# Step-wise inverses and layer norm, and projections that pass once over their weights, in a hybrid DeltaNet and sliding-window block

## The chip, the cores and the metric
One core of one Trainium2 chip (trn2). The metric is the device time of one execution in microseconds, as the median of several runs. The profile was taken in an execution of its own.

## The reference, cut to what matters
One post-norm block on x (1, 2048, 1024) in float32. Two token mixers read the same projections: a gated DeltaNet with 4 heads of 128 (chunks of the delta rule with a triangular inverse), and sliding-window attention with 8 query heads of 64 (window 128, rotation of the first quarter of each head). Both are gated, projected, merged, projected once more, added to the input and layer-normalized.

```python
h = einsum("bsd,dc->bsc", x, w_in)
t_inv = triangular_solve(eye + lower, eye)
u = t_inv @ (v * beta); w = t_inv @ (k_beta * exp(g))
def step(state, xs):
    v_new = u_i - w_i @ state
    o_i = qd_i @ state + a_i @ v_new
    state = state * exp(gl_i) + kt_i.T @ v_new
q_b = partial_rope(sw_q, cos, sin)
y_b = banded_sink_attention(q_b, k_b, v_b, sinks) * silu(sw_z)
merged = sigmoid(gate_a) * (y_a @ w_branch[0]) + sigmoid(gate_b) * (y_b @ w_branch[1])
r = DEEPNORM_ALPHA * x + merged @ w_out
y = (r - mean(r)) * rsqrt(var(r) + LN_EPS) * ln_g + ln_b
```

## The kernel before, in words
The 2048 tokens are worked on in four chunks of 512 (T), each of four blocks of 128 (NB). Every large product is made of three matmuls (L175, L176, L177 in `prods`): both operands are split into a high and a low part, and the product of the two low parts is dropped. The weights come as tiles `wb` of 512 KB (high and low part), in four buffers; in chunk 0 they are loaded raw and split by ScalarE (L156) and GpSimd (L157), and kept in DRAM as `kw_...` (one name for each kind: `kw_q` query, `kw_o` output projection, `kw_h` heads, `kw_g` gates), from which later chunks load them (L152).

The order of the work on TensorE is written by hand. A string names the pieces of a chunk ("kv k0 k1 q0 v0 p p p q1 p g w0 v1 z0 ... w1 v3 ..."), which are dense projections: `q0` projects queries of DeltaNet head 0, `p` is a quarter of the output projection of the chunk before (`project`), `w0` and `w1` are the query projections of the window attention (`window_q`) with two gate projections each, `g` is a gate. Between their matmuls a small planner (class `Order`) sets the steps of sparse tasks. It has a virtual clock, `st.now`, which each step moves on by what it costs TensorE. A task that was spawned runs again when its latency has passed on that clock; `until` lets a task wait for another one, and `finish` moves the clock on to whichever task is due, with no dense work in between, until the named task is done. The queues of the other engines are ordered by the scheduler, from the order in which the code emits.

The sparse tasks of a head: `front` (transposes L389 and products up to the matrix `m2`, whose diagonal parts go to DRAM and come back as `su`, L400 to L402); `inverse` (32x32 triangular inverses on VectorE: a memset at L905 as the first reader of `su`, then L908 to L910 and 16 pairs L916/L917; the result goes out at L425); `levels` (loads it back as `p_`, L437, and builds up the large inverse, first matmul L449); `back`, the delta chain (L496 matmul S k, L498 `bt` on VectorE, L501/L504 matmuls, L503 `wc` on VectorE, L507/L509 matmuls, L508 new state `S` on VectorE, and again for each of four blocks); `delta_gate`. For the window attention `query_rows` transposes the rotated queries (L564), and `attend` uses them.

`window_q` and `project` go twice over their weights: a first pass over two blocks loads four `wb` tiles and keeps them, a second pass over the other two blocks uses them again. `window_q` rotates the queries of two blocks behind each pass (`rope`, L866 to L868 on VectorE). `project` adds the input (L681); after the last quarter `layer_norm` of the chunk before is emitted as a whole: statistics on VectorE (L699), the normalization on ScalarE (L701), scale and shift on GpSimd (L708, L709) with parameters loaded as `s` (L705), and the store (L712). The layer norm of the last chunk has code of its own.

Of the kernel before, what the change touches and what calls it, by code (L numbers as in the profile page):

```python
# [16 lines left out]
P = 128  # L17
D = 1024
KT = D // P
T = 512  # L20
# [41 lines left out]
def build(tc, xt, xn, wk, wg, par, lnp, cst, out, seq=2048):  # L62
    nc = tc.nc
    NCH = seq // T
    with ExitStack() as ctx:
# [103 lines left out]

        def prods(ps, terms, first=True, last=True):  # L170

            n = len(terms) - 1
            cost = PE_R * ps.free_size() / 512
            for i, (sh, sl, mh, ml) in enumerate(terms):
                nc.tensor.matmul(ps, sh, mh, start=(first and i == 0), stop=False)  # L175
                nc.tensor.matmul(ps, sh, ml, start=False, stop=False)  # L176
                nc.tensor.matmul(ps, sl, mh, start=False, stop=(last and i == n))  # L177
                if cost * 3 * (i % 2 + 1) > 1000 or i == n:
                    yield cost * 3 * (i % 2 + 1)
# [12 lines left out]
        def prod_tc(pss, blocks, ah, al, ww, load=None):  # L192

            for g, (wh, wl) in enumerate(ww):
                if load:
                    load(2 * g + 1)
                for ps, b in zip(pss, blocks):
                    yield from prods(ps, [(tok(ah[2 * g + k], b), tok(al[2 * g + k], b), wh[:, k], wl[:, k])
                                          for k in range(2)], g == 0, g == 3)

        def kept(ww, into):
# [221 lines left out]
        def inverse(h, su, xi):  # L423
            small_inverse(tc, pt.tile([P, 256], F32, name="xt"), su, xi.rearrange("p (c i) -> p c i", i=32))
            nc.sync.dma_start(out=at(scr_p[h % 2], 0, [[P, P], [1, P]]), in_=xi)  # L425
            yield 0, 0

        def levels(c, h, m2, q_):

            yield from st.until(f"front{h}")  # L430
            if h:
                yield from st.until(f"levels{h - 1}")
            p_ = pt.tile([P, NB, 64], F32, name="p_")
            nc.gpsimd.memset(p_[:32, :, 32:], 0.0)
# [105 lines left out]
        def window_q(c, gp):  # L540

            if gp:
                st.finish("window0")
            c.qT = [pa.tile([P, NB, 2, P], F32R, name=n, bufs=1) for n in ("qT0", "qT1")]
            ww, more = [], quarters([f"q{gp}{i}" for i in range(2)])
            for b0 in (0, 2):
                pss = [mm.tile([P, T], F32, name="mm")[:, :256] for _ in range(2)]
                yield from prod_tc(pss, (b0, b0 + 1), c.xh, c.xl, ww if b0 else kept(more, ww), lambda k: load_x(c, k))
                if b0:
                    st.finish("qT0")  # L550
                qr = [pa.tile([P, 256], F32, name="kr") for _ in range(2)]
                for b, ps in enumerate(pss):
                    rope(nc, sm, qr[b], ps, 4, cos[:, c.i * NB + b0 + b], sin[:, c.i * NB + b0 + b])
                st.spawn(f"qT{b0}", query_rows(c, b0, qr), LAT_Q)
            for g in range(2):
                yield from silu2(c, f"zb{2 * gp + g}")
            st.spawn(f"window{gp}", attend(c, gp), LAT_W)
# [15 lines left out]
        def attend(c, gp):  # L573
            for b0 in (0, 2):
                yield from st.until(f"qT{b0}")
            if not gp:
                c.yBh = py.tile([P, 4, T], F32R, name="yBh")
                c.yBl = py.tile([P, 4, T], F32R, name="yBl")
# [88 lines left out]
        def project(c, eg):  # L667

            if not eg:
                c.ra = [py.tile([P, 2, D], F32, name=n) for n in ("yBh", "yBl")]  # L670
            ww, more = [], quarters([f"o{eg}{i}" for i in range(2)])
            es = slice(256 * eg, 256 * eg + 256)
            xr, pss = [], [mm.tile([P, 2, 256], F32, name="mm") for _ in range(2)]
            for bp in range(2):
                xr.append(pa.tile([P, 2, 256], F32, name="s"))
                t0 = c.i * T + bp * 256
                nc.sync.dma_start(out=xr[bp], in_=xn[t0:t0 + 256, es].rearrange("(b p) e -> p b e", p=P))
            for b2 in range(2):
                yield from prod_tc([ps[:, b2] for ps in pss], (b2, 2 + b2), c.mh, c.ml, ww if b2 else kept(more, ww))
            for bp in range(2):  # L680
                nc.vector.scalar_tensor_tensor(c.ra[bp][:, :, es], xr[bp], 2.0 * ALPHA, pss[bp], ALU.mult, ALU.add)  # L681

        def norm_factors(c, bst):
            mv = sm.tile([P, 2], F32, name="mv")
            nc.vector.bn_aggr(mv, bst)
            va = sm.tile([P, 1], F32, name="va")
            nc.vector.tensor_scalar(va, mv[:, 1:2], 4.0e-5, None, ALU.add)
            rs = sm.tile([P, 1], F32, name="rs")
            rsqrt(nc, sm, rs, va, mhalf)
            nm = sm.tile([P, 1], F32, name="lnm")  # L690
            nc.vector.scalar_tensor_tensor(nm, mv[:, 0:1], -1.0, rs, ALU.mult, ALU.mult)
            return rs, nm

        def layer_norm(c):
            for b in range(NB):
                r = c.ra[b // 2][:, b % 2]
                bst = sm.tile([P, 4, 6], F32, name="st", bufs=1)[:, :2]
                for i in range(2):
                    nc.vector.bn_stats(bst[:, i], r[:, 512 * i:512 * i + 512])  # L699
                rs, nm = norm_factors(c, bst)  # L700
                nc.scalar.activation(r, r, AF.Identity, scale=rs, bias=nm)  # L701
            for eg in range(4):
                es = slice(256 * eg, 256 * eg + 256)
                lg = pa.tile([P, 2, 256], F32, name="s")
                nc.sync.dma_start(out=lg, in_=bass.AP(tensor=lnp.tensor, offset=lnp.offset + 256 * eg, ap=[[0, P], [D, 2], [1, 256]]))  # L705
                for bp in range(2):
                    r = c.ra[bp][:, :, es]
                    nc.gpsimd.tensor_tensor(r, r, lg[:, 0:1].to_broadcast([P, 2, 256]), ALU.mult)  # L708
                    nc.gpsimd.tensor_tensor(r, r, lg[:, 1:2].to_broadcast([P, 2, 256]), ALU.add)  # L709
            for bp in range(2):  # L710
# [49 lines left out]
        def piece(c, w):  # L760
# [6 lines left out]
            elif w == "p":  # L767
                e = next(c.projects)
                st.dense([project(c.prev, e)])
                if e == 3:  # L770
                    layer_norm(c.prev)
            elif w[0] == "w":
# [33 lines left out]
class Order:  # L806

    def __init__(self):  # L810
        self.now, self.tasks, self.done = 0.0, [], set()
# [5 lines left out]
    def step(self, t):  # L817
        try:
            dur, lat = next(t[2])
        except StopIteration:  # L820
            self.done.add(t[1])
            self.tasks.remove(t)
            return
        self.now += dur
# [74 lines left out]
def small_inverse(tc, t, su, xi):  # L899
# [6 lines left out]
    for m in range(0, 16, 8):  # L906
        ms = slice(m, m + 8)
        nc.vector.tensor_tensor(tm, rows[:, ms, 1], view(su, 66 * m + 1, [[66, 8], [0, 32]]), ALU.mult)  # L908
        nc.vector.tensor_tensor(rows[:, ms, 0], rows[:, ms, 0], tm, ALU.add)
    nc.vector.memset(view(su, 0, [[33, 32]]), 1.0)  # L910
    tx = t.rearrange("p (c r k) -> p c r k", r=2, k=32)
    for i in range(30, -1, -2):
# [3 lines left out]
        nc.vector.tensor_tensor(tx[:, :, :, :n], u, x, ALU.mult)  # L916
        nc.vector.tensor_reduce(xi[:, :, i:i + 2], tx[:, :, :, :n], AX.X, ALU.add)  # L917


# [72 lines left out]
```

## Time and profile before

| what | value |
|---|---|
| median of 3 runs | 1720.17 us (1720.06 to 1723.12) |
| profiled execution | 1723.25 us |
| its span | 1721.5 us |
| mean granted TensorE clock | 0.983 of full speed |
| TensorE busy | 1631.3 us, 95% of the span |
| VectorE busy | 1020.2 us, 59% |
| ScalarE busy | 547.8 us, 32% |
| GpSimd busy | 374.2 us, 22% |
| DMA | 323.39 MB, 188 GB/s in the mean |

The profile shows one execution. PE is TensorE, DVE is VectorE, ACT is ScalarE, POOL is GpSimd, SP the engine whose queue issues most transfers; L12 is line 12 of the kernel. In a row of a timeline the first number is the start in microseconds from the start of the span, the second the duration, and the square brackets at the end give the idle time of the engine before it and what ended it. The releaser of a wait is inferred from semaphore events.

### The profile page before, as it was taken

How to read it: one execution, taken by the hardware profiler on the slowest of the kernel's cores; microseconds unless marked ns; L12 is line 12 of the kernel's file. 1: busy time of each engine (PE TensorE's matmuls, PEld its weight loads, DVE VectorE, ACT ScalarE, POOL GpSimd, SP SyncE). 2: the span in 40 equal slices, each digit the busy share in tenths (PEclk: the TensorE clock that was granted, in tenths of full speed). 3: DMA queues.
4: the chain of work that ended last, by engine and by line, in shares of the span. 5: the costliest groups of instructions: out<-in, count | busy, mean ns of one | idle time of the engine just before them, and what ended most of it. 6: DMA issues, size and time to landing. Idle time of an engine off the chain costs nothing.

```text
span 1721.5 us, 27328 instructions
## 1 busy us (share of the span) xinstructions
PE 1631.3 (95%) x9846; PEld 1372.2 (80%) x9846; DVE 1020.2 (59%) x3118; ACT 547.8 (32%) x1496; POOL 374.2 (22%) x366
## 2 busy tenths in 40 slices
PE   8989999999897999999989899999998989999997
PEld 6867878778886878888888687888888868888787
DVE  5677678446757756435546765643554867463245
ACT  3454445333232532321303243323130334333100
POOL 4543454341334111010003311100010521100002
PEclk9999999999999999999999999999999999999999
DMA  8765675667685455557555645556656554464862
GB/s 301 241 219 193 209 245 190 216 204 237 204 251 186 130 168 167 142 165 240 176 167 172 205 133 159 159 152 191 190 167 213 176 168 142 145 189 141 279 204 80
DMA packets 189159, 323.39 MB, mean 188 GB/s; under 512 B 31072, under 2 KB 45408, under 8 KB 188896
## 3 DMA queue, kind: packets, MB, share of 16 engines
q1 hardware_dynamic: 185184, 316.40, 58.3%
q0 software_dynamic: 3840, 5.25, 1.4%
q8 instruction: 78, 1.28, 0.3%
q14 instruction: 57, 0.47, 0.1%
HBM read 244.97 MB, written 71.37 MB: 184 GB/s over the span
## 4 chain that ended last, share of the span: by engine, by line
PE 71%; DVE 13%; DMA 9%; issue 3%; ACT 2%; SPq 1%; POOL 1%; ACTq 0%; DVEq 0%; POOLq 0%
PE mm L175 19%; PE mm L177 18%; PE mm L176 18%; DVE xt L916 2%; DMA wb<-kw_o 2%; PE pp L627 2%; DVE kr L867 2%; PE pp L619 1%; DVE xi L917 1%; DMA w<-in_wg 1%; DMA su<-scrm 1%; DMA wb<-kw_kv 1%; PE pp L588 1%; PE pp L589 1%; PE pd L501 1%
## 5 line engine op out<-in xcount | busy, mean ns | idle before, releaser
L175 PE MATMUL mm<-xh,wb 128*128 128x512 f32 x1128 | 474.4, 421 | 0.9 <-DMA wb<-kw_h 0.9
L177 PE MATMUL mm<-xh,wb 128*128 128x512 f32 x1128 | 447.1, 396 | 0.0
L176 PE MATMUL mm<-xl,wb 128*128 128x512 f32 x1128 | 446.2, 396 | 0.0
L177 PEld LDWEIGHTS mm<-xh,wb 128*128 128x128 f32 x1128 | 213.5, 189 | 50.2
L175 PEld LDWEIGHTS mm<-xh,wb 128*128 128x128 f32 x1128 | 214.6, 190 | 44.6 <-issue 5.7
L176 PEld LDWEIGHTS mm<-xl,wb 128*128 128x128 f32 x1128 | 215.2, 191 | 35.6
L157 POOL TENSOR_TENSOR wb<-w,wb 128x512 fp32r<-128x512 f32 (+1 forms) x110 | 149.7, 1362 | 193.2 <-ACT wb L156 171.2
L175 PE MATMUL mm<-wb,s 128*128 128x256 f32 x384 | 113.2, 295 | 18.7 <-DMA wb<-kw_o 12.9
L175 PE MATMUL mm<-wb,xh 128*128 128x256 f32 (+1 forms) x384 | 115.1, 300 | 11.0 <-DVE rope L866 4.2
L176 PE MATMUL mm<-wb,s 128*128 128x256 f32 x384 | 109.9, 286 | 1.0 <-POOL wb L157 1.0
L176 PE MATMUL mm<-wb,xh 128*128 128x256 f32 (+1 forms) x384 | 110.1, 287 | 0.3 <-POOL wb L157 0.3
L177 PE MATMUL mm<-wb,s 128*128 128x256 f32 x384 | 109.7, 286 | 0.0
L177 PE MATMUL mm<-wb,xl 128*128 128x256 f32 (+1 forms) x384 | 109.6, 285 | 0.0
L156 ACT ACTIVATE wb<-w 128x512 fp32r<-128x512 f32 (+1 forms) x110 | 68.8, 629 | 115.8 <-PE mm L177 55.7
L916 DVE TENSOR_TENSOR xt<-su,xi 128x16 f32<-128x16 f32 (+15 forms) x256 | 99.4, 388 | 5.5
L175 PEld LDWEIGHTS mm<-wb,s 128*128 128x128 f32 x384 | 74.4, 194 | 22.9 <-DMA wb<-kw_o 15.4
L605 ACT ACTIVATE s<-s,nm 128x256 f32<-128x256 f32 (+1 forms) x128 | 62.7, 491 | 82.6 <-DVE nm L599 82.6
L175 PEld LDWEIGHTS mm<-wb,xh 128*128 128x128 f32 x384 | 74.0, 193 | 14.3 <-issue 6.3
L917 DVE TENSOR_REDUCE xi<-xt 128x8 f32<-128x16 f32 (+15 forms) x256 | 74.6, 291 | 5.9
L176 PEld LDWEIGHTS mm<-wb,s 128*128 128x128 f32 x384 | 74.3, 194 | 1.6 <-POOL wb L157 1.5
L176 PEld LDWEIGHTS mm<-wb,xh 128*128 128x128 f32 x384 | 74.0, 193 | 0.9 <-POOL wb L157 0.6
L177 PEld LDWEIGHTS mm<-wb,s 128*128 128x128 f32 x384 | 74.2, 193 | 0.0
(666 smaller groups left out, 3165.4 us busy)
## 6 DMA issues: line engine op xcount, KB each, us to landing
wb<-kw_h SPq DMA_DIRECT2D x96, 512.0 KB, 4.1
wb<-kw_g SPq DMA_DIRECT2D x96, 512.0 KB, 4.0
w<-in_wg SPq DMA_DIRECT2D x106, 256.0 KB, 4.1
wb<-kw_b SPq DMA_DIRECT2D x48, 512.0 KB, 4.6
wb<-kw_o SPq DMA_DIRECT2D x36, 512.0 KB, 4.9
kw_h<-wb SPq DMA_DIRECT2D x32, 512.0 KB, 3.9
kw_g<-wb SPq DMA_DIRECT2D x32, 512.0 KB, 3.4
wb<-kw_q SPq DMA_DIRECT2D x24, 512.0 KB, 4.0
```

Source lines behind the costliest of these rows:

```text
L156: nc.scalar.activation(hi, raw, AF.Copy)
L157: nc.gpsimd.tensor_tensor(lo, raw, hi.bitcast(F32), ALU.subtract)
L175: nc.tensor.matmul(ps, sh, mh, start=(first and i == 0), stop=False)
L176: nc.tensor.matmul(ps, sh, ml, start=False, stop=False)
L177: nc.tensor.matmul(ps, sl, mh, start=False, stop=(last and i == n))
L501: nc.tensor.matmul(ps, q_[:, b], bt, start=True, stop=True)
L588: nc.tensor.matmul(psc[v][:, g, k0:], c.qT[v][:, b, g], kT[v][:, ks], start=True, stop=False)
L605: nc.scalar.activation(s[:, g, k0:], s[:, g, k0:], AF.Exp, bias=nm[:, g:g + 1], scale=0.125, accum_out=su[:, g:g + 1])
L627: nc.tensor.matmul(psY[64 * v:64 * v + 64], c.vs[b + kb][:, 64 * v:64 * v + 64], pTs[v][:, kb], start=(kb == kbs[0]), stop=(kb == 1))
L867: nc.vector.tensor_tensor(d[:, :, 0:8], a[:, 0, :, 0], a[:, 1, :, 1], ALU.subtract)
L916: nc.vector.tensor_tensor(tx[:, :, :, :n], u, x, ALU.mult)
L917: nc.vector.tensor_reduce(xi[:, :, i:i + 2], tx[:, :, :, :n], AX.X, ALU.add)
```

## The change
Four things change.

- `prod_all` takes the place of the two passes in `window_q` and `project`. It goes once over the weights; for each tile it runs over the four blocks in the order 0, 2, 1, 3, with two blocks open in each of two PSUM banks.
- In `window_q` the ropes of all blocks and both spawned `query_rows` come after the whole projection. `st.finish("qT0")` stands directly behind the spawning of qT0, which is due 7.9 us later on the virtual clock (LAT_Q).
- `inverse` and `layer_norm` yield after each step with `None` as cost, by which the virtual clock is not moved, and a latency after which the next step is emitted. `levels` waits for `inverse`, and `attend` for `norm`.
- `layer_norm` (chunks 0 to 2, run in chunks 1 to 3) applies its factors with 32 `scalar_tensor_tensor` of 128x256 on VectorE, in place of 4 activations on ScalarE and 16 instructions of 128x512 on GpSimd.

```diff
+        def prod_all(pss, ah, al, ww, load=None):
+            for g, (wh, wl) in enumerate(ww):
+                if load:
+                    load(2 * g + 1)
+                for b in (0, 2, 1, 3):
+                    yield from prods(pss[b // 2][:, b % 2], [(tok(ah[2 * g + k], b), tok(al[2 * g + k], b), wh[:, k], wl[:, k])
+                                                             for k in range(2)], g == 0 and not b % 2, g == 3, True)
...
         def inverse(h, su, xi):
-            small_inverse(tc, pt.tile([P, 256], F32, name="xt"), su, xi.rearrange("p (c i) -> p c i", i=32))
+            yield from small_inverse(tc, pt.tile([P, 256], F32, name="xt"), su, xi.rearrange("p (c i) -> p c i", i=32))
             nc.sync.dma_start(out=at(scr_p[h % 2], 0, [[P, P], [1, P]]), in_=xi)
-            yield 0, 0
+            yield None, 0
         def levels(c, h, m2, q_):
...
+            yield from st.until(f"inverse{h}")
...
             c.qT = [pa.tile([P, NB, 2, P], F32R, name=n, bufs=1) for n in ("qT0", "qT1")]
-            ww, more = [], quarters([f"q{gp}{i}" for i in range(2)])
+            pss = [mm.tile([P, 2, 256], F32, name="mm") for _ in range(2)]
+            yield from prod_all(pss, c.xh, c.xl, quarters([f"q{gp}{i}" for i in range(2)]), lambda k: load_x(c, k))
             for b0 in (0, 2):
-                pss = [mm.tile([P, T], F32, name="mm")[:, :256] for _ in range(2)]
-                yield from prod_tc(pss, (b0, b0 + 1), c.xh, c.xl, ww if b0 else kept(more, ww), lambda k: load_x(c, k))
                 if b0:
                     st.finish("qT0")
                 qr = [pa.tile([P, 256], F32, name="kr") for _ in range(2)]
-                for b, ps in enumerate(pss):
-                    rope(nc, sm, qr[b], ps, 4, cos[:, c.i * NB + b0 + b], sin[:, c.i * NB + b0 + b])
+                for b in range(2):
+                    rope(nc, sm, qr[b], pss[b0 // 2][:, b], 4, cos[:, c.i * NB + b0 + b], sin[:, c.i * NB + b0 + b])
                 st.spawn(f"qT{b0}", query_rows(c, b0, qr), LAT_Q)
...
             if not gp:
+                if c.i:
+                    yield from st.until("norm")
...
-            for b2 in range(2):
-                yield from prod_tc([ps[:, b2] for ps in pss], (b2, 2 + b2), c.mh, c.ml, ww if b2 else kept(more, ww))
+            yield from prod_all(pss, c.mh, c.ml, quarters([f"o{eg}{i}" for i in range(2)]))
...
-                rs, nm = norm_factors(c, bst)
-                nc.scalar.activation(r, r, AF.Identity, scale=rs, bias=nm)
+                rs, mu = norm_factors(c, bst, NB)
+                fs.append((r, rs, mu))
+                yield None, 2500
...
-                for bp in range(2):
-                    r = c.ra[bp][:, :, es]
-                    nc.gpsimd.tensor_tensor(r, r, lg[:, 0:1].to_broadcast([P, 2, 256]), ALU.mult)
-                    nc.gpsimd.tensor_tensor(r, r, lg[:, 1:2].to_broadcast([P, 2, 256]), ALU.add)
+                for r, rs, mu in fs:
+                    nc.vector.scalar_tensor_tensor(r[:, es], r[:, es], mu, lg[:, 0], ALU.subtract, ALU.mult)
+                    nc.vector.scalar_tensor_tensor(r[:, es], r[:, es], rs, lg[:, 1], ALU.mult, ALU.add)
+                    yield None, 1800
...
-                    layer_norm(c.prev)
+                    st.spawn("norm", layer_norm(c.prev), 0)
...
     def step(self, t):
...
+        if dur is None:
+            t[0] += lat
+            return
```

In `small_inverse` a `yield None, 1800` stands after each of the two steps L908/L909, and a `yield None, 420 + 40 * n` after each of the 16 pairs L916/L917 (n is 2, 4, ... 32).

The lines move with the change: L175 to L177 become L176 to L178, L496 L507, L498 L509, L501 L512, L503 L514, L504 L515, L507 L518, L508 L519, L509 L520, L564 L574, L866 to L868 L884 to L886, L905 L923, L908/L909 L926/L927. The two instructions of the new layer norm are L721 and L722.

How instructions move, at three places. First, TensorE in chunk 2, at the end of the query projection of w1 (the 128x256 matmuls are the projection, those of 128x512 a gate projection, `pd` are products of the delta chain, `pp<-ct,kr` the transposes of the rotated queries). Before:

```order
L175 MATMUL mm<-wb,xh 128x256
L176 MATMUL mm<-wb,xh 128x256
L177 MATMUL mm<-wb,xl 128x256
L564 MATMUL pp<-ct,kr 128x128 x4
L175 MATMUL mm<-xh,wb 128x512
L176 MATMUL mm<-xl,wb 128x512
L177 MATMUL mm<-xh,wb 128x512
...
L501 MATMUL pd<-bt,q__10757 128x128
L504 MATMUL pd<-S,qd 128x128
L175 MATMUL mm<-xh,wb 128x512
```

With the change:

```order
L177 MATMUL mm<-wb,xh 128x256
L178 MATMUL mm<-wb,xl 128x256
L507 MATMUL pd<-S,k 128x128
L512 MATMUL pd<-bt,q__10764 128x128
L515 MATMUL pd<-S,qd 128x128
L518 MATMUL pd<-wc,ktl 128x128
L520 MATMUL pd<-wc,dt 128x128
L507 MATMUL pd<-S,k 128x128
L574 MATMUL pp<-ct,kr 128x128 x4
L176 MATMUL mm<-xh,wb 128x512
```

The steps of a block of the chain and the transposes now stand behind each other, with no dense matmul in between. In w0 of chunks 1 to 3 five such products stand ahead of the transposes. Farther on, the first L449 of head 1 (during w0's gate projections and what follows) stands behind 30 dense 512-wide matmuls since the query projection, where it stood behind 54; L449 of head 3 (after w1) also moves up by about 24.

Second, VectorE at the same place (`rope` and `kr` are the rotations, `su` the inverse's input). Before:

```order
L516 TENSOR_SCALAR qsum<-qsum 128x4
L508 SCALAR_TENSOR_TENSOR S<-S,eGl,pd 128x128
L416 TENSOR_TENSOR dt<-pd,dt 128x512
L498 SCALAR_TENSOR_TENSOR bt<-pd,neG,vt 128x128
L905 MEMSET su 128x16
L908 TENSOR_TENSOR xt<-su 128x256
L909 TENSOR_TENSOR su<-su,xt 128x8x32
L866 TENSOR_TENSOR rope<-mm,ct 128x64 x2
```

With the change:

```order
L519 SCALAR_TENSOR_TENSOR S<-S,eGl,pd 128x128
L426 TENSOR_TENSOR dt<-pd,dt 128x512
L923 MEMSET su 128x16
L926 TENSOR_TENSOR xt<-su 128x256
L884 TENSOR_TENSOR rope<-mm,ct 128x64 x2
L927 TENSOR_TENSOR su<-su,xt 128x8x32
L509 SCALAR_TENSOR_TENSOR bt<-pd,neG,vt 128x128
L885 TENSOR_TENSOR kr<-rope 128x4x8
L886 TENSOR_TENSOR kr<-rope 128x4x8
L926 TENSOR_TENSOR xt<-su 128x256
L884 TENSOR_TENSOR rope<-mm,ct 128x64 x2
L514 TENSOR_SCALAR wc<-pd,cc 128x128
```

The `bt` of the chain stood ahead of the memset that waits for `su` and now stands behind it, as all four ropes do (before, the first pair of blocks had been rotated earlier).

Third, VectorE in w0 of chunk 1, with the change (`yBh` and `yBl` are the two halves of the rows that are normalized, `s` the parameters; before there were no such instructions on VectorE, and between `bt` and `wc` stood steps of the inverse):

```order
L721 SCALAR_TENSOR_TENSOR yBl<-yBl,mv,s 128x256
L722 SCALAR_TENSOR_TENSOR yBh<-yBh,rs,s 128x256
L509 SCALAR_TENSOR_TENSOR bt<-pd,neG,vt 128x128
L721 SCALAR_TENSOR_TENSOR yBh<-yBh,mv,s 128x256 x2
...
L935 TENSOR_TENSOR xt<-su,xi 128x8x2
L722 SCALAR_TENSOR_TENSOR yBl<-yBl,rs,s 128x256
L884 TENSOR_TENSOR rope<-mm,ct 128x64 x2
L722 SCALAR_TENSOR_TENSOR yBh<-yBh,rs,s 128x256
L514 TENSOR_SCALAR wc<-pd,cc 128x128
```

Here 17 of the 32 new instructions stand between the inverse's first step and its second pair, and instructions of the chain and a rope stand among them.

## Rows read from the trace of the kernel before

**Rows 1.** The page, engines: busy us (share of the span) x instructions.
```profile
PE 1631.3 (95%) x9846; PEld 1372.2 (80%) x9846; DVE 1020.2 (59%) x3118; ACT 547.8 (32%) x1496; POOL 374.2 (22%) x366
```
**Rows 2.** The page, costliest groups, output projections: busy, mean ns | idle before, releaser.
```profile
L175 PE MATMUL mm<-wb,s 128*128 128x256 f32 x384 | 113.2, 295 | 18.7 <-DMA wb<-kw_o 12.9
```
**Rows 3.** Waits of PE: us in total, times, longest us.
```profile
PE pd L501 <- DVE bt L498: 19.5, 7, 6.3
```
**Rows 4.** Windows: stretch, its us, busy us of PE, PEld, DVE, ACT, POOL, clock, DMA share, GB/s.
```profile
441.00:484.00 43.00, 35.44 (x262) 34.05 (x262) 22.22 (x54) 7.79 (x18) 13.75 (x11) 0.92 0.71 230
864.00:913.00 49.00, 41.82 (x306) 39.42 (x305) 21.41 (x58) 3.43 (x11) 0.00 (x0) 0.97 0.63 199
921.00:974.00 53.00, 44.24 (x270) 38.35 (x270) 42.84 (x111) 11.61 (x24) 26.20 (x26) 0.90 0.56 168
1286.00:1332.00 46.00, 40.09 (x306) 37.75 (x305) 20.43 (x56) 3.43 (x11) 1.04 (x1) 1.00 0.69 212
```
**Rows 5.** Timeline of PE, output projections in chunks 1 and 2.
```profile
457.46 0.58 PE L175 MATMUL mm<-wb,s 128*128 128x256 f32 x1 [5.61 <-ACT wb L156]
...
879.31 0.28 PE L176 MATMUL mm<-wb,s 128*128 128x256 f32 x1
879.43 0.28 PE L177 MATMUL mm<-wb,s 128*128 128x256 f32 x1
```
**Rows 6.** Timeline of PE, w0 of chunk 2, to L449 of head 1.
```profile
941.79 0.55 PE L175 MATMUL mm<-wb,xh 128*128 128x256 f32 x1 [1.40 <-DVE rope L866]
...
964.39 0.80 PE L501 MATMUL pd<-bt,q__9191 128*128 128x128 f32 x2 [6.29 <-DVE bt L498]
...
972.85 0.39 PE L175 MATMUL mm<-xh,wb 128*128 128x512 f32 x1
973.08 0.39 PE L176 MATMUL mm<-xl,wb 128*128 128x512 f32 x1
...
973.85 0.21 PE L449 MATMUL pd<-p__10093,m 32*32 32x32 f32 x1
```
**Rows 7.** Timeline of DVE, w0 of chunk 2.
```profile
935.36 0.07 DVE L905 MEMSET su<- 128x16 f32 x1
...
936.50 1.41 DVE L909 TENSOR_TENSOR su<-su,xt 128x256 f32<-128x256 f32 x1
...
952.95 0.18 DVE L868 TENSOR_TENSOR kr<-rope 128x32 f32<-128x32 f32 x1
...
956.10 6.99 DVE L867 TENSOR_TENSOR kr<-rope 128x32 f32<-128x32 f32 x1
...
964.70 0.42 DVE L917 TENSOR_REDUCE xi<-xt 128x8 f32<-128x256 f32 x1
```
**Rows 8.** Timeline of SP's queue after the inverse; DMA view: KB each, us to landing.
```profile
965.15 0.35 SPq L425 DMA_DIRECT2D scrp<-xi  x1
...
966.77 1.76 SPq L437 DMA_DIRECT2D p__10093<-scrp  x4
...
p__10093<-scrp SPq DMA_DIRECT2D x4, 16.0 KB, 3.3
```
**Rows 9.** Timeline of POOL, w0 of chunk 2, layer norm.
```profile
951.69 1.29 POOL L708 TENSOR_TENSOR yBh<-yBh,s 128x512 f32<-128x512 f32 x1 [5.59 <-DMA s<-in_lnp]
...
961.77 1.26 POOL L709 TENSOR_TENSOR yBl<-yBl,s 128x512 f32<-128x512 f32 x1
```
**Rows 10.** Groups of DVE by shape: busy us, mean ns | idle before.
```profile
L321 DVE SCALAR_TENSOR_TENSOR k<-xs,k 128x512 f32<-128x512 f32 x16 | 11.9, 742 | 5.8 <-ACT xs L320 5.8
```
**Rows 11.** Timeline of DVE and PE, w1 of chunk 2.
```profile
1091.46 0.07 DVE L905 MEMSET su<- 128x16 f32 x1 [2.67 <-DMA su<-scrm]
...
1088.97 0.60 PE L564 MATMUL pp<-ct,kr 128*128 128x128 f32 x4
```
**Rows 12.** Timeline of PE, end of chunk 0, chain without cover.
```profile
334.36 0.39 PE L496 MATMUL pd<-S,k 128*128 128x128 f32 x2
...
337.05 0.49 PE L496 MATMUL pd<-S,k 128*128 128x128 f32 x2 [0.22 <-DVE S L508]
```

More of the change, by code (lines that the diff above doesn't have):

```diff
@@ L168, in quarters, with prods @@
                     yield half_w(name, i, 2)
-        def prods(ps, terms, first=True, last=True):
+        def prods(ps, terms, first=True, last=True, shared=False):
             n = len(terms) - 1
@@ L174, in prods @@
             for i, (sh, sl, mh, ml) in enumerate(terms):
-                nc.tensor.matmul(ps, sh, mh, start=(first and i == 0), stop=False)
-                nc.tensor.matmul(ps, sh, ml, start=False, stop=False)
-                nc.tensor.matmul(ps, sl, mh, start=False, stop=(last and i == n))
+                nc.tensor.matmul(ps, sh, mh, start=(first and i == 0), stop=False, skip_group_check=shared)
+                nc.tensor.matmul(ps, sh, ml, start=False, stop=False, skip_group_check=shared)
+                nc.tensor.matmul(ps, sl, mh, start=False, stop=(last and i == n), skip_group_check=shared)
                 if cost * 3 * (i % 2 + 1) > 1000 or i == n:
@@ L670, in project @@
                 c.ra = [py.tile([P, 2, D], F32, name=n) for n in ("yBh", "yBl")]
-            ww, more = [], quarters([f"o{eg}{i}" for i in range(2)])
             es = slice(256 * eg, 256 * eg + 256)
@@ L677, in project, with norm_factors @@
                 nc.sync.dma_start(out=xr[bp], in_=xn[t0:t0 + 256, es].rearrange("(b p) e -> p b e", p=P))
-            for b2 in range(2):
-                yield from prod_tc([ps[:, b2] for ps in pss], (b2, 2 + b2), c.mh, c.ml, ww if b2 else kept(more, ww))
+            yield from prod_all(pss, c.mh, c.ml, quarters([f"o{eg}{i}" for i in range(2)]))
             for bp in range(2):
                 nc.vector.scalar_tensor_tensor(c.ra[bp][:, :, es], xr[bp], 2.0 * ALPHA, pss[bp], ALU.mult, ALU.add)
-        def norm_factors(c, bst):
-            mv = sm.tile([P, 2], F32, name="mv")
+        def norm_factors(c, bst, bufs=None):
+            mv = sm.tile([P, 2], F32, name="mv", bufs=NB)
             nc.vector.bn_aggr(mv, bst)
@@ L687, in norm_factors @@
             nc.vector.tensor_scalar(va, mv[:, 1:2], 4.0e-5, None, ALU.add)
-            rs = sm.tile([P, 1], F32, name="rs")
+            rs = sm.tile([P, 1], F32, name="rs", bufs=NB)
             rsqrt(nc, sm, rs, va, mhalf)
+            if bufs:
+                return rs, mv[:, 0:1]
             nm = sm.tile([P, 1], F32, name="lnm")
@@ L694, in layer_norm @@
         def layer_norm(c):
+            fs = []
             for b in range(NB):
@@ L909, in small_inverse @@
         nc.vector.tensor_tensor(rows[:, ms, 0], rows[:, ms, 0], tm, ALU.add)
+        yield None, 1800
     nc.vector.memset(view(su, 0, [[33, 32]]), 1.0)
@@ L917, in small_inverse @@
         nc.vector.tensor_reduce(xi[:, :, i:i + 2], tx[:, :, :, :n], AX.X, ALU.add)
+        yield None, 420 + 40 * n
 def tables(seq):
```

## The prediction
> **What bounds the kernel now.** The page first: TensorE is busy for 95% of the span [rows 1], so whatever leaves it idle, or at half clock, is what a change can win or lose. The profiled execution took 1723.25 us, 3.1 over the median of the runs (1720.17). I make the sum in its terms and take the 3.1 off at the end. Second, the page's costliest groups: the output projections (`wb,s`, 384 of each of three kinds in chunks 1 to 3) have 18.7 us of idle time ahead of their first kind of matmul, mostly behind loads of their weights [rows 2]. Third, the waits: 19.5 us of TensorE waiting for `bt` of the delta chain [rows 3]. Fourth, the table of stretches: the clock. In the output projections of chunks 1, 2 and 3 it is 0.92, 0.97 and 1.00, and 0.90 around the query projection w0 of chunk 2 [rows 4]. The clock has two levels, 1.2 and 2.4 GHz, so 0.92 over 43 us is about 7 us at the lower one.
>
> **Output projection, once over its weights.** Before, a pass takes 12 matmuls of 0.118 us from a 512 KB tile and goes on to the next, with four tiles to load in a pass of 5.7 us; TensorE then waits up to 5.61 us [rows 5]. Now a tile serves 24 matmuls, 2.85 us, and goes free. Of the 18.7 us [rows 2] I keep 3 (the first tile of a piece). The half clock in these stretches is 0.08 x 43 x 2 = 6.9 us in chunk 1, 0.03 x 49 x 2 = 2.9 in chunk 2 and none in chunk 3; half of that is lost time, 4.9 us, of which I give back 4.5. Term A: -15.7 - 4.5 = **-20**, from -10 (half of the waits stay) to -24.
>
> **The query projection in w0 (chunks 1 to 3).** Two things change together. On TensorE, the rotations now come after all four blocks, and the emission clock jumps to the first transposes: what lay between the two passes as filler is gone, and head 1's first level matmul (L449) stands 24 dense 512-wide matmuls earlier, 24 x 0.231 = 5.5 us (0.231 from one start to the next, as at 972.85 and 973.08 [rows 6]), some 6 with the small products among them. That work isn't lost: it comes after L449, so it costs only if L449 can't run then. Can it? In chunk 2, L449 begins at 973.85, behind waits of 1.40 and 6.29 us [rows 6]. The inverse needs `su` (first step 935.36) and ends at 965.12 [rows 7]; its result goes out and comes back as `p_`, a store issued at 965.15, loads from 966.77, 3.3 us to landing [rows 8], so it is usable 6 us after the inverse's end. TensorE with 6 us less ahead of L449, and without these 7.7 us of waits, would be there at 973.9 - 6 - 7.7 = 960. To cost nothing, the inverse would have to end at 954.
>
> Why did it end at 965? It has 11 us of work (my sum over its 38 instructions, the first 0.07 and the last 0.42 us [rows 7]). From 936.50 to 956.10, seven VectorE instructions run longer than others of their shape; the longest is a 128x32 subtraction of 6.99 us, where one of the same shape takes 0.18 [rows 7]. My sum over the seven is 12.5 us. All lie where GpSimd works too, and the 6.99 us end as GpSimd's last layer-norm instruction does (961.77 + 1.26) [rows 9]. So with that work gone VectorE gets up to 12.5 us back; GpSimd's 16 instructions a chunk, at 1.26 to 1.29 us [rows 9], are 20.4. In their place stand 32 instructions of 128x256. The nearest row, the same operation on 128x512, takes 742 ns [rows 10], so 0.36 each, 11.5 a chunk. In the order shown 17 of them, 6.1 us, stand between the inverse's first step and its second pair, among `bt`, `wc`, `S` and the ropes, on which TensorE waits; one waits for its parameters (GpSimd waited 5.59 us for such a load [rows 9]). From 935.4: 11 (inverse) + 6.1 + about 6 (ropes, `S`, `bt`, the norm's small operations) + 0 to 3 for the load, and some waits for TensorE because queue order ties them: 961 to 966. I take 963.5, L449 at 969.5. Against 973.85 that is -4.4, then +6 of moved work, and +2.8 because idle stretches here were followed by half clock (0.90 over 53 us [rows 4]). Term B: +4 a chunk, from -3 to +9: **+12**. The removed activations of ScalarE (32% busy) cost and save nothing: TensorE does not wait for them.
>
> So the rows give back 12.5 us at most and take 11.5 for the new instructions: an even trade on VectorE, and not one for the inverse, whose queue now has the norm in front. A rule bears on that trade. The Trainium skill ("SBUF — State Buffer", section "Who interferes with whom") says that a VectorE instruction with two SBUF inputs and a GpSimd instruction that reads SBUF exclude each other, and the loser is blocked for the whole instruction. The trace agrees as far as the 6.99 us go, but an instruction of that kind at 952.95 took its usual 0.18 us with GpSimd in the middle of the norm [rows 7, 9]. If all 20.4 us came back, as the rule would have it at its strictest, the inverse would end near 955, B would be about -2 a chunk, and the sum 1717; by the rows' 12.5 it is the 1735 below.
>
> **The query projection in w1 (chunks 1 to 3).** Before, block by block, `bt` and a first pair of ropes stand ahead of the inverse's first step, a memset that waits for `su` to land. That wait, to 1091.46, costs TensorE nothing: it works on the second pass and the transposes at 1088.97, and on the next projection [rows 11]. In the new VectorE order `bt` and all four ropes stand behind that memset, and on TensorE the chain steps L507 (S k), L512/515 (`bt`), L518/520 (`wc`), L507 and the transposes L574 follow each other with no projection between. The projection ends about 1088.8; `bt` comes at 1091.46 + 1.7 (five instructions ahead), three hops follow. A hop without cover: one block, L496 to L496, takes 337.05 - 334.36 = 2.69 us for three hops [rows 12], 0.9 each. So dense work is back at 1091.5 + 1.7 + 2.7 + 1.0 = 1096.9, 8.1 us after the projection, of which 1.5 is TensorE's own work on these steps: 6.6 idle, 5.5 where the ropes overlap. With half clock behind it, by what the 6.29 us wait brought in w0: +1.5. Term C: +7 a chunk (3 to 9): **+20**. L449 of head 3 also stands 6 us of work earlier; the idle time in w1 delays TensorE by as much, so I add nothing.
>
> **Chunk 0.** The same w1 without a layer norm: 1.8 idle, L449 5 us late: +6; its tail gets a fourth uncovered block of the delta chain, 2.7 us less what it replaces: +2; w0 +1. Term D: **+9** (2 to 12). The rest (skip_group_check, buffers for the norm's factors, an earlier store of the output) I cost at nothing: the first is no instruction, the others are covered by dense work; without it they'd cost a few tenths of a us. Other waits of TensorE behind VectorE may shorten: -3 (0 to -8).
>
> **Sum**: -20 + 12 + 20 + 9 - 3 = +18 to 1723.3, 1741; with the 3.1 off, 1738. I take 3 off for waits counted in both B and C: **1735 us**, +15.
>
> **Rivals.** R1, faster: VectorE, free of GpSimd, ends the inverse before TensorE comes to L449 (by 954 in chunk 2), and `su` lands before the projection ends in w1 (1091.46 against 1088.8 must turn round: 3 us). For it: the 12.5 us [rows 7], and steps spread out so that `bt`, `wc` and `S` slip between them. Against: the order with the new instructions ahead of the ropes. Then A stays, the 6.29 us waits go, C and D are small: -20 - 3 x 3 + 2 = -27, **1693 us**. R2, the parts cancel: B is -3 a chunk, C +3, D +9 and the rest -3: -20 - 9 + 9 + 9 - 3 = -14; with C at +7 and B at 0 it is +7; a time within 0.2% (3.4 us, about what a measurement can tell here) lies between. R3, worse: the output projection's loads come no earlier (the tiles of the next piece wait as before), A is -10, B +9 and C +9 a chunk, D +12: -10 + 27 + 27 + 12 = +56, less 4: **1772 us**; it decides where the new memset-and-parameter waits exceed 6 us. R4, the change doesn't do what it says: the output projection is bound by the DMA queue, not by tiles held, and A is -2 to -10, in the middle 14 us less than -20, with 2 us of it eased in B: **1747 us**. Against it: the waits come at the start of a first pass, when four tiles are held.
>
> **How the numbers follow.** Forecast and its neighbours (slower, 1724 to 1760) 0.44, R1 0.34, R2 0.10, R3 and R4 together 0.12. So faster by over 0.2% 0.34, same 0.10, slower 0.56. The range takes in the forecast's, R2, R4 and R1's from 1690 up, so 1690 to 1766; the forecast's own is 1724 to 1760.
>
> **What would show it.** Right: idle of `wb,s` matmuls under 5 us in the groups; in w1 a wait of TensorE for `bt`, `wc` and a rope of 5 us in all after the query projection; L449 of head 1 waiting for `p_`. Wrong: `su` landed and ropes done before the projection's end, no memset ahead of `bt` in time, L449 without waits, clock 1.00 over w0.

## The result, and the profile after

The change made the kernel slower: 1766.89 us (median of 4, 1763.72 to 1769.16) against 1721.24; ratio 1.0258, 95% interval 1.0244 to 1.0273. The profiled execution has a span of 1767.3 us, 45.8 more than before, at a mean granted clock of 0.966 (0.983 before). The page, engines, against [rows 1]:

```profile
PE 1651.1 (93%) x9846; PEld 1391.7 (79%) x9846; DVE 1022.9 (58%) x3202; ACT 538.1 (30%) x1484; POOL 314.7 (18%) x318
```

TensorE is busy for 20 us longer with the same 9846 matmuls, and idle time has grown by 26 us (1767.3 - 1651.1 against 1721.5 - 1631.3). The 20 us fit the clock: a mean of 0.966 over 1767.3 us is 120 us at the lower of its two levels, 0.983 over 1721.5 us is 59, and the 61 us more would cost 31 if TensorE had been busy all that time. In the output projections idle time went from 18.7 to 6.3 us (the forecast kept 3 of it, and its sign of being right was under 5). All but one of their waits are gone, and that one is not for weights but for VectorE, as the page's group shows beside [rows 2]:

```profile
L176 PE MATMUL mm<-wb,s 128*128 128x256 f32 x384 | 111.1, 289 | 6.3 <-DVE yBh L691 6.3
```

TensorE's waits (engine, line <- releaser: us in total, times, longest), against [rows 3]:

```profile
PE pd L512 <- DVE bt L509: 16.7, 14, 4.0
PE pd L518 <- DVE wc L514: 10.7, 8, 3.1
PE pd L495 <- DVE v L331: 9.2, 3, 3.1
PE pd L460 <- DMA p__10045<-scrp: 6.7, 1, 6.7
PE pd L460 <- DMA p__14238<-scrp: 6.3, 1, 6.3
...
PE pd L460 <- DMA p__5852<-scrp: 5.7, 1, 5.7
```

L460 is the first level matmul (L449 before); it now waits for `p_`, as does, a little later, L495, the first matmul of head 1's delta chain, for `v`. Before, L449 waited 0.6 us at most, and L484, which is now L495, not at all.

Where the 45.8 us lie is read from windows between the first transposes of successive heads, which are the same piece of work in each kernel. Length of each stretch in us, chunks 1 to 3 added up:

| stretch | before | change | difference |
|---|---|---|---|
| chunk 0, to chunk 1 head 0 | 432.8 | 445.5 | +12.7 |
| head 0 to 1 (output projection) | 173.9 | 153.9 | -20.0 |
| head 1 to 2 (w0) | 287.5 | 311.5 | +24.0 |
| head 2 to 3 | 183.0 | 181.2 | -1.8 |
| head 3 to the next chunk or the end (w1, gates, branches) | 644.3 | 675.2 | +30.9 |

Windows of w0 and of the stretch from head 3 on, chunk 2, first before, then the change (columns as in [rows 4]):

```profile
913.70:1010.10 96.40, 87.64 (x577) 74.58 (x574) 70.28 (x207) 30.41 (x83) 31.46 (x32) 0.95 0.55 170
1071.10:1278.00 206.90, 206.35 (x1140) 171.96 (x1140) 105.47 (x342) 59.31 (x165) 15.38 (x21) 1.00 0.58 176
```
```profile
928.90:1033.00 104.10, 88.13 (x578) 75.28 (x573) 70.63 (x241) 26.53 (x79) 10.72 (x16) 0.93 0.50 154
1093.40:1313.60 220.20, 213.55 (x1149) 177.20 (x1148) 104.97 (x342) 60.38 (x165) 15.37 (x21) 0.97 0.56 165
```

In w0 the idle time of TensorE goes from 8.8 to 16.0 us; from head 3 on from 0.6 to 6.7, and the clock falls from 1.00 to 0.97, which on 220 us is worth up to 6.6. TensorE in the change, w0 of chunk 2, where [rows 6] had waits of 1.40 for a rope and 6.29 for the chain's `bt`, and then w1:

```profile
965.22 0.38 PE L518 MATMUL pd<-wc,ktl 128*128 128x128 f32 x1 [3.06 <-DVE wc L514]
...
985.18 0.31 PE L460 MATMUL pd<-p__10045,m 32*32 32x32 f32 x2 [6.71 <-DMA p__10045<-scrp]
...
1008.47 0.30 PE L495 MATMUL pd<-ct,v 128*128 128x128 f32 x1 [3.05 <-DVE v L331]
...
1115.40 0.49 PE L512 MATMUL pd<-bt,q__10764 128*128 128x128 f32 x2 [3.25 <-DVE bt L509]
...
1142.81 0.24 PE L460 MATMUL pd<-p__11579,m 32*32 32x32 f32 x2 [1.88 <-DMA p__11579<-scrp]
```

VectorE in the change at the same places, against [rows 7, 11]: the inverse of head 1 begins and ends, with one wait for the norm's parameters between; then the inverse of head 3 begins, with the chain's `bt` behind it.

```profile
954.56 0.07 DVE L923 MEMSET su<- 128x16 f32 x1
...
959.05 0.88 DVE L721 SCALAR_TENSOR_TENSOR yBh<-yBh,mv,s 128x256 f32<-128x256 f32 x2 [1.69 <-DMA s<-in_lnp]
...
981.36 0.42 DVE L936 TENSOR_REDUCE xi<-xt 128x8 f32<-128x256 f32 x1
...
1113.96 0.07 DVE L923 MEMSET su<- 128x16 f32 x1 [2.75 <-DMA su<-scrm]
...
1115.00 0.34 DVE L509 SCALAR_TENSOR_TENSOR bt<-pd,neG,vt 128x128 f32<-128x128 f32 x1
```

Counted from head 1's first transposes (913.68 before, 928.92 now), the inverse begins after 25.6 us (21.7 before) and ends at 52.9 (51.4 before). Its end is hardly later than it was. What moved is L449/L460 on TensorE: before, it came 60.2 us after these transposes and did not wait; now TensorE stands ready for it at 49.6 and waits 6.71 us. The lower clock lies at such waits: 0.50 was granted from 965.6 to 972.4, behind the wait for `wc`, and 0.51 from 982.6 to 989.5, around the wait for `p_`.

### The profile page after: what moved, and what is told of

It reads as the page before. It is cut to its first block, busy times and chain, and to the rows that moved or that the text cites. A ratio compares the mean times of both kernels' runs of the same rounds, so it can differ in the third digit from the quotient of the medians.

```text
span 1767.3 us, 27284 instructions
## 1 busy us (share of the span) xinstructions
PE 1651.1 (93%) x9846; PEld 1391.7 (79%) x9846; DVE 1022.9 (58%) x3202; ACT 538.1 (30%) x1484; POOL 314.7 (18%) x318
## 4 chain that ended last, share of the span: by engine, by line
PE 75%; DVE 12%; DMA 8%; ACT 2%; issue 1%; SPq 1%; POOL 1%; ACTq 0%; DVEq 0%; POOLq 0%
PE mm L176 20%; PE mm L177 19%; PE mm L178 19%; PE pp L639 2%; DMA su<-scrm 2%; PE pp L631 2%; DMA s<-in_lnp 1%; DVE xt L935 1%; DMA scrp<-xi 1%; PE pd L518 1%; PE pd L507 1%; PE pd L399 1%; PE pp L600 1%; DVE xi L936 1%; DVE q L328 1%
## 5 line engine op out<-in xcount | busy, mean ns | idle before, releaser
L176 PE MATMUL mm<-xh,wb 128*128 128x512 f32 x1128 | 476.3, 422 | 0.1
L178 PE MATMUL mm<-xh,wb 128*128 128x512 f32 x1128 | 451.5, 400 | 0.0
L177 PE MATMUL mm<-xl,wb 128*128 128x512 f32 x1128 | 451.2, 400 | 0.0
L176 PEld LDWEIGHTS mm<-xh,wb 128*128 128x128 f32 x1128 | 218.4, 194 | 49.4 <-issue 8.1
L178 PEld LDWEIGHTS mm<-xh,wb 128*128 128x128 f32 x1128 | 216.4, 192 | 51.8
L177 PEld LDWEIGHTS mm<-xl,wb 128*128 128x128 f32 x1128 | 218.5, 194 | 39.1
L176 PE MATMUL mm<-wb,xh 128*128 128x256 f32 (+1 forms) x384 | 113.6, 296 | 5.8 <-DVE ba L274 3.2
L176 PE MATMUL mm<-wb,s 128*128 128x256 f32 x384 | 111.1, 289 | 6.3 <-DVE yBh L691 6.3
L177 PE MATMUL mm<-wb,xh 128*128 128x256 f32 (+1 forms) x384 | 109.1, 284 | 0.3 <-POOL wb L157 0.3
L177 PE MATMUL mm<-wb,s 128*128 128x256 f32 x384 | 109.0, 284 | 0.0
L178 PE MATMUL mm<-wb,s 128*128 128x256 f32 x384 | 108.9, 284 | 0.0
L178 PE MATMUL mm<-wb,xl 128*128 128x256 f32 (+1 forms) x384 | 108.9, 284 | 0.0
L935 DVE TENSOR_TENSOR xt<-su,xi 128x16 f32<-128x16 f32 (+15 forms) x256 | 92.4, 361 | 5.9
L176 PEld LDWEIGHTS mm<-wb,s 128*128 128x128 f32 x384 | 73.7, 192 | 8.0 <-DVE yBh L691 6.5
L176 PEld LDWEIGHTS mm<-wb,xh 128*128 128x128 f32 x384 | 73.0, 190 | 8.2 <-issue 5.0
L177 PEld LDWEIGHTS mm<-wb,xh 128*128 128x128 f32 x384 | 73.0, 190 | 0.9 <-POOL wb L157 0.6
L177 PEld LDWEIGHTS mm<-wb,s 128*128 128x128 f32 x384 | 73.6, 192 | 0.1
L178 PEld LDWEIGHTS mm<-wb,s 128*128 128x128 f32 x384 | 73.4, 191 | 0.0
```

Source lines behind the costliest of these rows:

```text
L177: nc.tensor.matmul(ps, sh, ml, start=False, stop=False, skip_group_check=shared)
```

## The experiments

Three theories stood against each other. **The jump**: behind the once-through query projection `finish` moves the virtual clock (also called the emission clock below) on by 7.9 us with no dense work in between, and that costs all of it, in two ways: L449 stands too early (1a), or the chain and the transposes stand without dense work around them, "without cover" (1b). **The norm**: layer norm on VectorE delays the inverse in w0. **The stepwise inverse**: emitting it step by step delays it.

**e1_output_only.** The kernel before, with `prod_all` in `project` alone.

```diff
-            for b2 in range(2):
-                yield from prod_tc([ps[:, b2] for ps in pss], (b2, 2 + b2), c.mh, c.ml, ww if b2 else kept(more, ww))
+            yield from prod_all(pss, c.mh, c.ml, quarters([f"o{eg}{i}" for i in range(2)]))
```

> The kernel before with one part of the change alone: the output projection goes once over its weights. Both theories (the cost of the change comes from the jump of the emission clock in the query projection; or from the layer norm on VectorE) let the output projection stand as the gain. By the stretches from head 0's to head 1's first transposes, which became 1.9, 10.5 and 7.6 us shorter in chunks 1 to 3 with the change, it should take 20 us off: 1701 us, and 1697 to 1706. A rival: those stretches got shorter only because what stood ahead of them got later; then the time stays within 5 us of 1721.

Measured: 1696.05 us, ratio 0.9857 [0.9841, 0.9873]. The output stretches come to 150.8 us (173.9 before), each other stretch is within 2 us of before. This part gains what was forecast, and no other run was faster.

**e2_two_pass_queries.** The change, with `window_q` as before.

```diff
-            yield from prod_all(pss, c.xh, c.xl, quarters([f"q{gp}{i}" for i in range(2)]), lambda k: load_x(c, k))
             for b0 in (0, 2):
+                pss = [mm.tile([P, T], F32, name="mm")[:, :256] for _ in range(2)]
+                yield from prod_tc(pss, (b0, b0 + 1), c.xh, c.xl, ww if b0 else kept(more, ww), lambda k: load_x(c, k))
```

> The change with the query projection in two passes, as before; output projection, inverse and layer norm as in the change. Theory 1 (the jump of the emission clock behind the once-through query projection costs w1, chunk 0 and most of w0): 31 us in w1, 13 in chunk 0 and 15 to 24 of w0 come back, 1767 - 60 to 68, so 1699 to 1707, and no wait of TensorE for bt or p_ over 3 us in w1. Theory 2 (the layer norm on VectorE costs w0, 24 us, and pushes on what follows): w0 stays 20 us or more over the kernel before, and the time is 1715 to 1730.

Measured: 1712.16 us, ratio 0.9952 [0.9936, 0.9969]: 55 us under the change. Chunk 0 is back at 433.5, w0 at 293.3, the stretch from head 3 on at 647.7. The query projection carries the loss. The time lies between the two ranges, 5 us above the first and 3 below the second; w0 is 6 us over the kernel before, not the 20 that the norm theory asked for. What is left over e1 is 16 us.

**e3_norm_on_scalar_gpsimd.** The change, with the layer norm as before.

```diff
-                    st.spawn("norm", layer_norm(c.prev), 0)
+                    layer_norm(c.prev)
```
(and `layer_norm` and `norm_factors` as before; `attend` doesn't wait for the norm)

> The change with the layer norm as before: on ScalarE and GpSimd, emitted as a whole; TensorE's order is that of the change. Theory 1: the uncovered chain and the early L449 stay, so within 8 us of the change: 1759 to 1775; in w0 the inverse is blocked by GpSimd again, so L449 may even come later. Theory 2: w0 comes back to its old length, 24 us less: 1738 to 1746.

Measured: 1768.20 us, ratio 1.0268 [1.0253, 1.0283]. The norm is not the cause: without it on VectorE the loss stays whole.

**e4_gate_between_ropes.** The change, with the first gate projection between the two pairs of ropes, so that the clock has nothing to jump over.

```diff
                 if b0:
+                    yield from silu2(c, f"zb{2 * gp}")
                     st.finish("qT0")
...
-                st.spawn(f"qT{b0}", query_rows(c, b0, qr), LAT_Q)
-            for g in range(2):
-                yield from silu2(c, f"zb{2 * gp + g}")
+                st.spawn(f"qT{b0}", query_rows(c, b0, qr), LAT_Q if b0 else 5000)
+            yield from silu2(c, f"zb{2 * gp + 1}")
```

> The change with one thing moved: the first gate projection of the piece stands between the ropes of blocks 0, 1 and those of blocks 2, 3, and the first transposes are due 5.0 us after, so that the emission clock doesn't jump; the projection still goes once over its weights. Theory 1: as with the query projection in two passes, 1697 to 1710, since only the jump goes. Theory 2: 1740 or more, w0 unchanged. A third possibility: that once over the weights itself costs something in the query projection (the filler between the passes is missed): then some 5 to 15 us over the run with two passes.

Measured: 1721.13 us, ratio 0.9998 [0.9978, 1.0017], the runs between 1710.03 and 1726.05; the profiled one is the fastest of them, so its stretches are not compared here. Without the jump 46 us come back; some 9 us over two passes remain, the third possibility.

**e8_queries_once_only, e7_norm_only, e6_inverse_only, e5_inverse_at_once.** Each part added to e1 by itself, and the change without the stepwise inverse. The edits are the diff's own hunks, taken or left: e8 is before with `prod_all` in both projections; e7 is e1 with the new `layer_norm` and its waits; e6 is e1 with the yields in `small_inverse` and the wait in `levels`; e5 is the change without these and without the yields in `small_inverse`:

```diff
-            yield from small_inverse(tc, pt.tile([P, 256], F32, name="xt"), su, xi.rearrange("p (c i) -> p c i", i=32))
+            small_inverse(tc, pt.tile([P, 256], F32, name="xt"), su, xi.rearrange("p (c i) -> p c i", i=32))
...
-            yield from st.until(f"inverse{h}")
```

> The kernel before with both projections once over their weights (the jump of the emission clock is in it), and inverse and layer norm as before. Against the run with the output projection alone (1696) this adds the query projection alone. Theory 1 (the jump is the cost, whatever the inverse and the norm do): 1696 + 46 to 60, so 1742 to 1756, with w1 7 to 13 us a chunk and w0 7 to 10 us a chunk longer than there. Rival (the jump only costs together with the stepwise inverse, whose steps stand among the chain on VectorE): 1700 to 1720.

> The run with the output projection alone (1696) plus the layer norm on VectorE as a task. With two passes the three parts together took 1712. If the norm is what makes up the 16 us between them: 1708 to 1714, with w0 1 to 4 us a chunk longer. If the stepwise inverse is: 1694 to 1699.

> The run with the output projection alone (1696) plus the inverse emitted a step at a time, for which the first level matmul now waits on the emission clock too. If the stepwise inverse makes up the 16 us: 1708 to 1714, with 2 to 3 us more in each w1, where there is no norm; if the norm does: 1694 to 1699. I expect it in between, 1700 to 1706.

> The change with the inverse emitted as a whole, as before; both projections once, the norm on VectorE. Theory 1 (the jump): 1757 to 1769, the stepwise inverse being worth 0 to 10 us. Rival (the stepwise inverse is what the jump exposes, since its input's landing now stands ahead of bt and the ropes on VectorE): 1715 to 1735.

Measured: e8 1765.61 us, ratio 1.0264 [1.0246, 1.0281], more than expected; e7 1709.27, 0.9934 [0.9917, 0.9951]; e6 1699.14, 0.9880 [0.9863, 0.9897], just below the 1700 to 1706 expected; e5 1764.87, 1.0260 [1.0236, 1.0283]. So over e1 the query projection alone costs 70 us, the norm 13, the stepwise inverse 3, which the intervals can't tell from nothing. With two passes the last two add up (1696 + 13 + 3 = 1712, as e2 measured); under the jump they cost nothing that can be told (e3, e5, e8 and the change lie within 4 us).

**e9_levels_later.** The change with one number changed, to tell 1a from 1b: L460 gets its cover back, the chain and the transposes stay without.

```diff
-            st.spawn(f"levels{h}", levels(c, h, m2, q_), max(LAT_B, t0 + LAT_INV - st.now))
+            st.spawn(f"levels{h}", levels(c, h, m2, q_), max(LAT_B, t0 + LAT_INV + 6000 * (h % 2) - st.now))
```
(and the same for `back`)

> The change with one number changed: the levels and the delta chain of heads 1 and 3 are due 6.0 us later on the emission clock, so that the first L449 of head 1 stands behind 54 dense matmuls after the query projection, as before, where the change has 30, and that of head 3 behind 96 where it has 72. The chain and the transposes behind each query projection stay without cover. Theory 1a (most of the jump's price is L449 coming too early, its wait for p_, the wait for v behind it and the half clock after them): 1725 to 1738. Theory 1b (most of it is the uncovered chain and its half clock): 1752 to 1767.

Measured: 1715.65 us, ratio 0.9958 [0.9939, 0.9978], 51 us under the change and 9 better than theory 1a gave it. Windows of e9, w0 and from head 3 on, chunk 2:

```profile
910.50:1002.00 91.50, 85.03 (x564) 72.27 (x563) 69.25 (x238) 26.19 (x79) 11.01 (x16) 0.96 0.58 176
1064.20:1274.90 210.70, 208.23 (x1141) 173.39 (x1141) 105.55 (x342) 60.12 (x165) 15.46 (x21) 0.99 0.58 173
```

and in its TensorE timeline, w0, the chain still waits for `wc` as in the change, but L460 hardly for `p_` (2.8 us in chunk 3 are the longest in a w0):

```profile
946.93 0.80 PE L518 MATMUL pd<-wc,ktl 128*128 128x128 f32 x2 [3.06 <-DVE wc L514]
...
967.09 0.24 PE L460 MATMUL pd<-p__10093,m 32*32 32x32 f32 x2 [0.48 <-DMA p__10093<-scrp]
```

w0 takes 91.5 us, less than before (96.4), with the norm on VectorE and the chain uncovered; 1.2 us of that went into the stretch behind it (62.17 for 60.93). From head 3 on it takes 210.7, 3.8 more than before. As e2, in which the chain has its cover, already takes 208.9 there, 1b is worth some 2 to 4 us in that stretch.

**e10_transposes_due_at_once.** The change with another number changed: the clock has no 7.9 us to jump over, and TensorE waits for the first ropes instead.

```diff
-                st.spawn(f"qT{b0}", query_rows(c, b0, qr), LAT_Q)
+                st.spawn(f"qT{b0}", query_rows(c, b0, qr), LAT_Q if b0 else 0)
```

> The change with one number changed: the first transposes of a query projection are due at once on the emission clock, in place of 7.9 us later, so that finish finds them due and the clock doesn't jump. They now stand right behind the projection and wait for the first pair of ropes. Theory 1 (the jump is the price, not the wait for a rope): some 2.5 us of wait in each of the 8 query projections, L449 with its cover back, 1712 + 20 = 1732, and 1720 to 1740. Rival (the ropes coming after the whole projection are the price): 1750 or more.

Measured: 1727.78 us, ratio 1.0024 [1.0006, 1.0042]. The jump, not the ropes' place, is the price; waiting for a rope in the open is far cheaper, though not free: it is 16 us over e2.

**e12_before_levels_earlier.** The converse: the kernel before, with nothing of the change, but L449 as early as the change has it.

```diff
-            st.spawn(f"levels{h}", levels(c, h, m2, q_), max(LAT_B, t0 + LAT_INV - st.now))
+            st.spawn(f"levels{h}", levels(c, h, m2, q_), max(LAT_B, t0 + LAT_INV - 5600 * (h % 2) - st.now))
```
(and the same for `back`)

> The kernel before, nothing of the change in it, with one number changed: levels and delta chain of heads 1 and 3 are due 5.6 us earlier on the emission clock, so that L449 stands behind 30 and 72 dense matmuls after the query projections, as in the change, where before has 54 and 102. Theory 1a (the early L449 is most of the price of the change): w0 +5 to 8 and w1 +5 to 8 us a chunk, some 4 in chunk 0, so 1721 + 25 to 50: 1746 to 1771. Rival (the early L449 hurts only together with the chain left without cover): 1721 to 1732.

Measured: 1795.80 us, ratio 1.0425 [1.0403, 1.0447], 75 us slower than before. In its trace L449 of heads 1 and 3 stands behind 30 and 72 dense matmuls in chunks 1 to 3, as in the change (54 and 102 before, so head 3's came forward by 30, not by the 24 counted ahead of the result). Its timeline of TensorE in w0 and w1 of chunk 2 has the change's waits, the one for `v` included, in a kernel without jump or new norm:

```profile
1001.64 0.31 PE L449 MATMUL pd<-p__10052,m 32*32 32x32 f32 x2 [4.88 <-DMA p__10052<-scrp]
...
1026.46 0.63 PE L484 MATMUL pd<-ct,v 128*128 128x128 f32 x4 [3.55 <-DVE v L321]
...
1158.76 0.31 PE L449 MATMUL pd<-p__11582,m 32*32 32x32 f32 x2 [5.82 <-DMA p__11582<-scrp]
```

w0 takes 319.5 us over the three chunks (before 287.5, change 311.5), from head 3 on 672.9 (644.3, 675.2). The 75 us are more than the change lost in all; but the change had 20 us back from the output projection, and without them it would be at 1787 (an estimate). `back` was moved with `levels`, so the run doesn't part the price of L449 from that of the wait for `v`. The expectation was too low by 25 us or more.

**e11_norm_output_levels_later.** A version of the good parts: e7 with levels and chain of head 1 due later.

```diff
+            st.spawn(f"levels{h}", levels(c, h, m2, q_), max(LAT_B, t0 + LAT_INV + 6000 * (h == 1) - st.now))
```
(and the same for `back`)

> A version made of what the runs showed to be good: output projection once over its weights, layer norm on VectorE (GpSimd off VectorE's back), query projection in two passes, inverse as before, and levels and chain of head 1 due 6.0 us later, since TensorE waited 6.7 to 7.1 us for p_ in each w0 of the run with output projection and norm (1709). If L449's place is what that wait hangs on: 1709 - 3 x 7 and up to 4 of half clock, so 1684 to 1692, below every run so far. If the waits only move to what comes behind L449: 1700 to 1709.

Measured: 1698.51 us, ratio 0.9865 [0.9845, 0.9884]; 11 us better than e7, not the 17 to 25 expected, and level with e1. w0 falls from 293.3 to 267.8 us over three chunks, the shortest of all; but 11 us of that come back between heads 2 and 3 (184.1 to 195.6), where the moved work now lies, and chunk 0 gets 9 longer. The fastest version is e1, at 1696.05; e11 can't be told from it.

## Why the prediction was right or wrong, point by point

The direction was right, the size wrong: 1735 was forecast, +15 over the median shown, and +46 was measured, just above the range's upper end of 1766. The 31 us between are 12 in B, 11 in C, 4 in D, and 4 of the 6 us that the sum took off for waits that would shorten or were counted twice: against those 6 stand only 1.8 us, between heads 2 and 3. The nearest rival by number (R3, 1772) had B, C and D nearly right (9 and 9 a chunk and 12, against 8.0, 10.3 and 12.7), but not its reason: A did not fail, and the waits for the norm's parameters took 1.9 us at most, not over 6. R4 falls with A's 20 us, and R2 needed B and C near nothing.

- **Term A, right**: -20 forecast, -20.0 in the stretches, of which -14.4 is idle time and -5.6 busy time (forecast -15.7 and -4.5); -25 in e1 by itself.
- **Term B (w0), direction right, size wrong**: +12 forecast, +24.0 measured. Its time for L449 fits: 55.8 us after the head's first transposes forecast, 985.18 - 928.92 = 56.3 measured. That is in part luck: the inverse ended 3.1 us later on this count than forecast (52.9 for 963.5 - 913.7 = 49.8), and its result was in use 3.4 us after its end, not 6. The step that failed is what was put behind L449: 6 us of moved work and 2.8 of clock, and no wait. From L449 to head 2's first transposes it took 36.3 us before and 47.8 now, 11.5 more. The `back` task of the same head is timed by the same clock, so it came early as well, and its L495 waited 3.05 us for `v`, in each chunk; another 0.8 us went at L460's next matmul. With some 2 us for the clock (0.51 up to 989.5) that leaves 5.5 for the moved work, which was sized right. I had counted what was moved ahead of L449, not who else is due by the clock that jumped.
- **Term C (w1), the clock mis-sized, and a wait put at nothing**: +20 forecast, +30.9 measured. Idle time grew by 15.8 us over the three chunks, where 3 x 5.5 was forecast; that this agrees is luck. The order's uncovered chain behind the memset was real, but cost 1.6 to 3.3 us a chunk at `bt` (3.25 in chunk 2), at most 0.35 at `wc` and nothing that shows at the rope, where I had three hops. The rest of the idle time is at L460, which waited 1.9 to 2.1 us a chunk for `p_`, and up to 1.3 more behind: the sentence "L449 of head 3 also stands 6 us of work earlier; ... so I add nothing" is wrong. TensorE's busy time grew by 15.1 us. The clock in these stretches is 0.99, 0.97 and 0.97 (1.00, 1.00 and 0.98 before), which is worth up to 11 us, where the forecast had 1.5 a chunk, 4.5. Some 2 us more is work that came over from the stretch before; the last 2 stay open.
- **Term D (chunk 0)**: +9 forecast, +12.7 measured.
- **The clock**, over all: the terms had it at +8 (4.5 back in A, 2.8 in each w0, 1.5 in each w1); TensorE's busy time grew by 20 us with the same matmuls. It falls at waits, and e9, where L460's are mostly gone, has 0.96 and 0.99 in the stretches of chunk 2 where the change has 0.93 and 0.97.
- **The norm on VectorE**: most of the blocked time came back. Before, a 128x32 subtraction of the ropes takes 956 ns in the mean, after it 205, which is 24 us over the kernel for this group alone:

```profile
L867 DVE TENSOR_TENSOR kr<-rope 128x32 f32<-128x32 f32 x32 | 30.6, 956 | 0.5
```
```profile
L885 DVE TENSOR_TENSOR kr<-rope 128x32 f32<-128x32 f32 x32 | 6.5, 205 | 0.2
...
L721 DVE SCALAR_TENSOR_TENSOR yBl<-yBl,mv,s 128x256 f32<-128x256 f32 x24 | 10.5, 472 | 0.0
```

 The new instructions take 0.47 us, not 0.36: half of a 128x512 was too little. The Trainium skill ("SBUF — State Buffer", section "Who interferes with whom") has a VectorE instruction with two SBUF inputs contend with a GpSimd instruction that reads SBUF. The 956 and 205 ns agree. But the gain of the strictest case did not come: the inverse would have ended near 955, 10 us earlier than before, and it ended 1.5 us later, counted from its head's first transposes, with the norm's instructions among its own. In e7, with two passes, moving the norm costs 13 us; TensorE waits 6.7 to 7.1 us for `p_` in each w0 there, and e11, where L449 is due later, has the 13 us back but for some 2.
- **R1** had its chance of 0.34 from the inverse being early. It was not.

What was the price of the uncovered chain in w0 alone, apart from L449, wasn't measured by itself: e9 also moves `back`.

## What to carry to other kernels

Where an order is written by a clock that a wait can move on, count every task that falls due in the jump and what each then waits for; one that comes too early costs its wait, the waits of the tasks chained to it, and the clock behind them. A term that says "it is only moved" has to be checked at the new place as a stall is. Here the output projection was worth -25 us, and on top of it the stepwise inverse +3, the norm +13 and the query projection +70, each alone: a change in four parts should be tried by parts.

## What was not expected of the hardware

The longer busy time, which fits the lower clock, came to three quarters of the new idle time: 20 us to 26, in a kernel whose TensorE is idle for 7% of the span. And runs of one kernel differ in the clock: e4's runs go from 1710.03 to 1726.05, at clocks of 0.983 down to 0.973.
